# One gate load in another pool with one more bank, and the up part begun seven pairs ahead in a written order

## The chip, the cores and the metric

The kernel runs on one core of one Trainium2 chip. The metric is the device time of one execution in microseconds (us). Engines run side by side: PE multiplies matrices, ACT (ScalarE) and DVE (VectorE) do elementwise work, POOL a little more of it, and SP issues most transfers. Each engine takes its instructions in order, and so does the queue from which SP issues. PE writes into PSUM, which has eight banks here, four under the name "at" and four under "mm"; everything else is in the on-chip memory SBUF or in DRAM.

## The reference

One decoder block in float32 on 1024 tokens (S) of 1024 features (D). What bears on the change:

```python
h = _rmsnorm(x, g_mix_pre)
proj = h @ w_in + b_in                       # u_pool, q, k, v, gates
...
g = sigmoid(gates)                           # 2048 columns
merged = g_pool * (y_pool @ w_branch_pool) + g_attn * (y_attn @ w_branch_attn)
x = x + _rmsnorm(merged @ w_out, g_mix_post)
h2 = _rmsnorm(x, g_mlp_pre)
ff = square(relu(h2 @ w_up)) @ w_down        # 4096 columns between
x = x + _rmsnorm(ff, g_mlp_post)
```

## The kernel before

**Three passes for one product.** A float32 operand is split into a high and a low part (`split`, L99): ACT casts the high part (L101), DVE subtracts it from the source (L104). A product of two operands is then three passes on PE: high by high, high by low, low by high. Wherever a text here says that an operand is made, that is one ACT cast and one DVE subtraction, after the sums that it needs.

**Pairs.** The gates (8 pairs) and the up part of the MLP (16 pairs) work on pairs of 128-column blocks of the weight, an even and an odd one, by a scheme with seven products of half size for eight (`Pairs`, L439). For pair p the products are numbered 1 to 7. `load` (L448) brings one block of weights, by default into a `stage` tile (pool "st", 3 buffers), else into the tile that is given. `operand(p, i)` (L453) makes weight operand i: 1 and 2 from the even block alone, 4 from the odd one, 5, 6, 7 and 3 after sums and differences on DVE (L459, L462, L466, L469). Operands lie in "wh" (6 buffers); 5, 6 and 7 of later pairs in "ga" (gates, 6 buffers) or "x1" (up part, 4 buffers). `mm` (L482) runs one product: 4 column groups by 3 passes, 12 matmuls into one bank. `m1` (L489) runs product 1 and copies the bank out on ACT (L493); `m2` (L495) adds product 2 on the same bank and closes it (a DVE multiplication in the gates, L675; an ACT Relu in the up part, L1071). `rest` (L500) runs 6, 7, 5, 4, 3 and adds on DVE what each gives (L507, L514, L518, L521 or L524, L527). In `rest`, product 4 is added onto the bank of product 7, and then may start only when DVE has read that bank (L514); if a bank `b4` is given, product 4 has that bank to itself and L524 adds it. Product 3 is added onto the bank of product 5 after L518 has read it.

**Order.** Instructions are put in order when the kernel is built: a list scheduler places each one by the order of the program and by when it expects its inputs. Inside a `manual_schedule` block the named engines keep the written order of the block's own instructions; others from outside the block can still be put between them.

**Gates.** Products 1 and 2 of all eight pairs come first, in a block that orders PE, DVE, ACT and SP (L852-L879), while DVE builds the four sums of the activations (T1 to T4) for the column groups kt = 1, 2, 3 (`build_gate`, L702) into "g" tiles (17 buffers). It also loads both blocks of pair 0. The loop at L892 then runs `rest` for p = 0 to 7; it loads the blocks of pair p at its head, the odd block into a "g" tile from p = 3 on and into a stage tile before. `rest(0)` writes into a fresh "y" tile (4 buffers) whose last holder is the result of a pair's products 1 and 2, stored to DRAM at L846.

**Output projection.** `out_mm(n)` (L996) multiplies token block n = 0 to 7 by `w_out`, 48 matmuls into two banks. `out_post(n)` (L1009) is the first norm (ACT squares at L982, then a chain of single-column operations, L1018 and L1019 on DVE) and stores x1; `out_norm(n)` (L1023) is the second, again with L982, and ends with L1027. The result x1 of a block stays in an "x1" tile. At n = 5 `build_first` (L1038) transposes blocks 0 to 3 on PE (L1035, eight groups of four into an "at" bank) and makes operands B11 and B21 from them; an ACT copy (L1045) keeps each group in float32.

**Start of the up part.** From L1157: pairs 0 to 4 are begun ahead (NF0 = 5). `build_second(kt)` (L1048) transposes blocks 4 to 7 for one column group (eight transposes, two banks), and from two banks makes T1 to T4 and B22: one ACT copy (L1056), four DVE operations (L1057-L1060) and five operands. The rest of pair 0 has products 6 and 7 interleaved by column group (`first_kt`), and its result is the tile `f_first`. This part has no written order. After it the loop at L1193 runs pairs 1 to 15: operands, the loads of the next pair, `m1` where it was not run ahead, `flush()` (the stores of the pair before), `rest`. A store (`store`, L1080) is four DVE operations (L1085-L1088) and three transfers to `f_dram`.

**Down part.** From L1322 the squares come back from `f_dram` for the last product. Its gain is `gfin_b` (L1138).

Of the kernel before, what the change touches and what calls it, by code (L numbers as in the profile page):

```python
# [14 lines left out]
P = 128  # L15
# [35 lines left out]
def block_kernel(ctx: ExitStack, tc, xt, x, consts, vecs, sinks, b_qkv, g_post, g_mlp, g_mlp_post,  # L51
# [16 lines left out]
    def nm(s):  # L68
        cnt[0] += 1
        return f"{s}_{cnt[0]}"  # L70
# [618 lines left out]
    def gate_result():  # L689
        return flat(yy.tile([P, 2, 512], F32, tag="y", name=nm("z")))  # L690
# [161 lines left out]
    with tc.manual_schedule(engines={mybir.EngineType.PE, mybir.EngineType.DVE, mybir.EngineType.Activation,  # L852
                                     mybir.EngineType.SP}):
        builds = later_builds()
        gt.load(6)
        gt.load(8)
        load_x(2, lambda: g32([S]))
        first(0)
        first(1)
        for p in range(NG0):  # L860
            if p + 3 < NG0:
                gt.operand(p + 3, 1)
            if p + 2 < NG0:
# [12 lines left out]
            if p + 5 < NG0:  # L876
                gt.load(2 * p + 10)
            elif p < 5:
                gt.load(p - 3)  # L879
    asp = [[None, None], [None, None]]  # L880

    def load_attn():
# [9 lines left out]
    for p in range(8):  # L892
        if NHELD <= p + 1 < 8:
            gt.f0[p + 1] = gate_result()
            nc.sync.dma_start(gt.f0[p + 1], z_dram[2 * p + 2])
        if p:
            gt.load(2 * p)
            gt.load(2 * p + 1, g32([NK, P]) if p > 2 else None)
        for i in (6, 7, 5, 4, 3) if p else (5, 4, 3):
            gt.operand(p, i)  # L900
        tag = "at" if p % 2 == 0 else "mm"
        gt.rest(p, gate_result(), bank(tag), bank(tag), bank(tag), then=load_attn if p == 7 else None)


    def gate_load(m):
# [103 lines left out]
    def out_post(n):  # L1009

        bs = obs.pop(n)
        xs = stage([D])
        nc.sync.dma_start(xs, x[n])
        t = xq.tile([P, D], F32, tag="x1", name=nm("x1"))
        r = mean_sq(bs, halves(t))
        for dj in range(2):
            sl = slice(dj * 512, (dj + 1) * 512)
            dve.scalar_tensor_tensor(t[:, sl], bs[dj], r, gpost_b[:, sl], ALU.mult, ALU.mult)  # L1018
        dve.tensor_tensor(t, t, xs, ALU.add)  # L1019
        nc.sync.dma_start(x1_dram[n], t)  # L1020
        hs[n] = t, xs
# [13 lines left out]
            pe.transpose(b[:, i, :], hs[4 * th + i][:, k * P:(k + 1) * P], ident)  # L1035
        return flat(b)

    def build_first():  # L1038
        for kt in range(4):
            raw[kt] = g32([2, 512])  # L1040
            for h, name in ((0, "B11"), (1, "B21")):
                b = tr_block(0, 4 * h + kt)
                t = gr([2, 512])
                split(t[:, 0, :], t[:, 1, :], b)
                act.copy(raw[kt][:, h, :], b)  # L1045
                X[name][kt] = t

    def build_second(kt):  # L1048
        b12, b22 = tr_block(1, kt), tr_block(1, 4 + kt)
        if kt % 2:  # L1050
            tmp = stage([2, 512])
        else:
            tmp = ga_.tile([P, 2, 512], F32, tag="ga", name=nm("tt"))
        r11, r21 = raw[kt][:, 0, :], raw[kt][:, 1, :]
        t3, t2 = tmp[:, 0, :], tmp[:, 1, :]
        act.copy(t3, b12)  # L1056
# [18 lines left out]
    def up_close0(m, f):  # L1075
# [4 lines left out]
        def store():  # L1080

            g = f_odd.pop(m + 1)
            t = g32([2, 512])
            s4 = bcp.tile([P, 1024], F32, tag="bc", name=nm("s4"))[:, :512]
            dve.tensor_tensor(t[:, 0, :], f[:, 512:], g[:, 512:], ALU.add)  # L1085
            dve.tensor_tensor(t[:, 1, :], t[:, 0, :], f[:, :512], ALU.subtract)
            dve.tensor_tensor(f[:, 512:], f[:, :512], f[:, 512:], ALU.subtract)
# [32 lines left out]
    out_norm(1)  # L1120
    for n in range(2, NT):
        if n == 5:
            out_mm(n, range(0))
            build_first()
            out_mm(n, range(0, NK))
        else:
            out_mm(n, range(NK))
        out_post(n)
        out_norm(n)
        if n == 5:  # L1130
            for p in range(3):
# [22 lines left out]
        h, dj = B_OF[name]  # L1154
        return w_rows[s_, h][:, :, dj * 512:(dj + 1) * 512]

    up.prepare(3)  # L1157
    up.prepare(4)
    up.load(0)
    up.load(1)  # L1160
    for p in range(4):
        up.m1(p, bank("mm"))

    def first_kt(kt):
        up.mm(b6, 0, 6, (kt,))
        up.mm(b7, 0, 7, (kt,))

    build_second(0)
    up.m2(0)
    up.m1(4, bank("mm"))  # L1170
    build_second(1)
    up.operand(0, 6)
    up.m2(1)
    b6, b7 = bank("at"), bank("at")
    build_second(2)
    for i in (7, 5, 4, 3):
        up.operand(0, i)
    up.m2(4)
    up.m2(2)
    first_kt(0)  # L1180
    build_second(3)
    up.m2(3)
    first_kt(1)
    first_kt(2)
    first_kt(3)
    def load_pair(p):
        up.load(2 * p)
        up.load(2 * p + 1, g32([NK, P]))
# [4 lines left out]
    for p in range(1, NP):  # L1193
# [257 lines left out]
```

## Time and profile before

| | |
|---|---|
| runs | 1133.22 us median of 3 (1132.43 to 1134.31) |
| profiled execution | 1132.83 us, its span 1131.0 us |
| mean granted PE clock | 0.998 |
| instructions | 13992 |
| DVE busy | 817.1 us (72%) |
| ACT busy | 523.3 us (46%) |
| DMA | 186.94 MB, mean 165 GB/s |

A row of the timeline has the start from the span's beginning, the time from the first start to the last end, engine, line, operation, tiles (out<-in) and count; in brackets, how long the engine was idle just before, and what released it. A row of windows has, for each engine, its busy time in that stretch and the number of instructions that touch it. "SPq" is a transfer being issued; a count on such a row spreads over its whole time. PE is the matmul, PEld the load of its stationary operand. A matmul's end is modelled, about 0.16 us after the next one may start, so the distance between starts says more than the busy time.

### The profile page before, as it was taken

To read this page: it belongs to the slowest core of one execution; us is meant where nothing else is said; L and a number is where in the kernel's file an instruction comes from. 1 tells how busy PE (TensorE), PEld (TensorE's weight loads), DVE (VectorE), ACT (ScalarE), POOL (GpSimd) and SP (SyncE) were. 2 spreads that over 40 slices of the span, in tenths; PEclk is the share of its full clock that TensorE was granted. 3 is DMA by queue.
4 is the path that set the end of the run, shared out by engine and by line. 5 is a ranking of instruction groups with operands and counts; after the bars stand their busy time and mean duration, and the time that the engine had idled before them with its cause. 6 is when DMAs were issued, how large, how long until landed. Compare 5 with 4: busy or idle time off the path is not lost.

```text
span 1131.0 us, 13992 instructions
## 1 busy us (share of the span) xinstructions
PE 1119.4 (99%) x5213; PEld 925.8 (82%) x5213; DVE 817.1 (72%) x1217; ACT 523.3 (46%) x911; POOL 50.1 (4%) x104
## 2 busy tenths in 40 slices
PE   9999999999999999999999999999999999999997
PEld 8888888878888888888788888888888888888885
DVE  7578897898855785678997666666557955446787
ACT  8265655454432333446555444444444345344342
POOL 0242100000000320000000000000000000000000
PEclk9999999999999999999999999999999999999999
DMA  8102338255664434243365343434597765332652
GB/s 282 50 1 93 113 130 316 100 207 213 224 230 142 162 136 150 97 146 112 141 223 205 138 161 144 157 142 161 214 345 260 244 206 193 100 95 73 223 191 89
DMA packets 72052, 186.94 MB, mean 165 GB/s; under 512 B 6448, under 2 KB 10672, under 8 KB 71984
## 3 DMA queue, kind: packets, MB, share of 16 engines
q1 hardware_dynamic: 66368, 166.38, 42.1%
q10 hardware_dynamic: 5616, 19.66, 4.5%
q8 instruction: 41, 0.67, 0.2%
q14 instruction: 27, 0.22, 0.1%
HBM read 132.54 MB, written 53.48 MB: 164 GB/s over the span
## 4 chain that ended last, share of the span: by engine, by line
PE 92%; DVE 5%; ACT 2%; DMA 1%; issue 1%; DVEq 0%
PE mm L486 22%; PE at L486 15%; PE at L1289 14%; PE mm L1289 12%; PE mm L1006 6%; PE mm L423 5%; PE mm L576 4%; PE mm L183 3%; PE mm L425 3%; PE at L395 2%; PE sc L334 1%; PE at L192 1%; PE sc L183 1%; PE at L1006 1%; PE mm L192 1%; PE at L377 1%
## 5 line engine op out<-in xcount | busy, mean ns | idle before, releaser
L1289 PE MATMUL at<-ar,wh 128*128 128x512 f32 x744 | 169.5, 389 | 0.0
L1289 PEld LDWEIGHTS at<-ar,wh 128*128 128x128 f32 x744 | 139.6, 188 | 29.3 <-DVE ar L104 0.4
L1289 PE MATMUL mm<-ar,wh 128*128 128x512 f32 x576 | 131.0, 389 | 0.0
L104 DVE TENSOR_TENSOR wh<-raw,wh 128x1024 fp32r<-128x1024 f32 x53 | 64.8, 1223 | 86.4 <-ACT wh L101 86.4
L1289 PEld LDWEIGHTS mm<-ar,wh 128*128 128x128 f32 x576 | 108.1, 188 | 22.5
L101 ACT CAST wh<-raw 128x1024 fp32r<-128x1024 f32 x53 | 55.8, 1053 | 135.6 <-PE at L1289 63.3
L101 ACT CAST wh<-st 128x512 fp32r<-128x512 f32 (+1 forms) x105 | 66.2, 642 | 110.4 <-PE at L486 31.0
L104 DVE TENSOR_TENSOR wh<-st,wh 128x512 fp32r<-128x512 f32 (+1 forms) x106 | 79.1, 757 | 21.2 <-ACT wh L101 18.7
L486 PE MATMUL mm<-gr,wh 128*128 128x512 f32 x300 | 72.3, 390 | 0.1
L486 PE MATMUL mm<-T,wx 128*128 128x512 f32 x288 | 67.5, 389 | 0.0
L486 PEld LDWEIGHTS mm<-gr,wh 128*128 128x128 f32 x300 | 56.0, 188 | 11.9 <-ACT g L1071 0.5
L486 PEld LDWEIGHTS mm<-T,wx 128*128 128x128 f32 x288 | 54.1, 188 | 11.2
L486 PE MATMUL at<-T,wx 128*128 128x512 f32 x252 | 59.1, 389 | 0.0
L486 PEld LDWEIGHTS at<-T,wx 128*128 128x128 f32 x252 | 47.3, 188 | 9.8
L486 PE MATMUL mm<-x,wh 128*128 128x512 f32 x240 | 55.2, 389 | 0.0
L486 PEld LDWEIGHTS mm<-x,wh 128*128 128x128 f32 x240 | 45.0, 188 | 9.4
L104 DVE TENSOR_TENSOR ar<-B,ar 128x1024 fp32r<-128x1024 f32 x37 | 45.1, 1219 | 5.6 <-ACT ar L101 5.3
L576 PE MATMUL mm<-x,wh 128*128 128x512 f32 x192 | 47.6, 396 | 0.0
L486 PE MATMUL at<-gr,wh 128*128 128x512 f32 x183 | 44.6, 390 | 0.0
L101 ACT CAST ar<-B 128x1024 fp32r<-128x1024 f32 x37 | 38.9, 1051 | 7.8 <-DMA B<-in_w_dn_dram 4.9
L576 PEld LDWEIGHTS mm<-x,wh 128*128 128x128 f32 x192 | 35.3, 188 | 7.7
L486 PEld LDWEIGHTS at<-gr,wh 128*128 128x128 f32 x183 | 34.3, 188 | 7.7 <-DVE gr L104 0.5
(367 smaller groups left out, 2163.2 us busy)
## 6 DMA issues: line engine op xcount, KB each, us to landing
raw<-f_dram SPq DMA_DIRECT2D x53, 512.0 KB, 3.6
f_dram<-g SPq DMA_DIRECT2D x30, 512.0 KB, 3.3
B<-in_w_dn_dram SPq DMA_DIRECT2D x24, 512.0 KB, 6.3
st<-in_w_up_dram SPq DMA_DIRECT2D x22, 512.0 KB, 3.5
st<-in_w_g_dram SPq DMA_DIRECT2D x19, 512.0 KB, 3.5
f_dram<-g ACTq DMA_DIRECT2D x17, 512.0 KB, 2.6
g<-spill_dram SPq DMA_DIRECT2D x16, 512.0 KB, 4.5
raw<-in_w_dn_dram SPq DMA_DIRECT2D x16, 512.0 KB, 4.5
```

The source lines that it names most:

```text
L101: act.copy(hi, src)
L104: eng.tensor_tensor(lo, src, f32(hi), ALU.subtract)
L183: pe.matmul(bq, xs_[k][n // 4][:, xh, n % 4 * P:(n % 4 + 1) * P], wq[k][:, h, :], start=k == 0 and j == 0, stop=k == NK - 1 and j == 2)
L192: pe.matmul(bkv_of(n), xs_[k][n // 4][:, xh, n % 4 * P:(n % 4 + 1) * P], wkv[k // 2][:, h, k % 2, :], start=k == 0 and j == 0 and not (joi ...
L334: pe.matmul(sb[:, kv, i, :nk], qt[r, qx, m * P:(m + 1) * P], kx[r, k0:k0 + nk], start=j == 0, stop=j == 2)
L395: pe.matmul(yb.rearrange("p m q -> p (m q)"), v[:, vh, kv * HD:kv * HD + P], p[ph][:, 4 * kv:4 * kv + 4].rearrange("p i q -> p (i q)"), st ...
L423: pe.matmul(bs[th], whi[:, k, :], rhs(k, hl, th), start=k == 0 and hl == 0, stop=False)
L425: pe.matmul(bs[th], wlo[:, k, :], rhs(k, 0, th), start=False, stop=k == nk - 1)
L486: pe.matmul(b, w[:, wh, kt, :], xo[kt][:, xh, :], start=not after and kt == 0 and j == 0, stop=kt == 3 and j == 2, skip_group_check=after)
L576: pe.matmul(b, (whi, wlo)[h][:, k, :], xr(k, xh, th), start=j == 0, stop=j == len(mms) - 1)
L1006: pe.matmul(obs[n][dj], l, wos[k][whl][:, dj * 512:(dj + 1) * 512], start=k == 0 and hl == 0 and whl == 0, stop=k == NK - 1 and hl == 1)
L1289: pe.matmul(bs[t], fo[fh][:, k2, t * P:(t + 1) * P], wo_[wh][:, k2, :], start=not after and s2 == 0 and k2 == 0 and j == 0, stop=s2 == NS ...
```

## The change

Gates: both blocks of pair 1 are loaded inside the ordered block at p = 6, the odd one into a "g" tile; the loop no longer loads them. Product 4 of pair 0 has a bank of its own.

Output projection: x1 of block 4 lies in a "g" tile instead of an "x1" tile. At n = 5 the matmuls and the transposes alternate, one eighth of each at a time, in written order on PE. The even block of pair 3 is loaded at n = 6, and the norms of block 7 move into the new block below.

Up part: pairs 0 to 6 are begun ahead (NF0 = 7). Everything from the norms of block 7 to products 6 and 7 of pair 0 is in one block with a written order for PE, DVE and ACT; SP is left to the scheduler. The first results of pairs 4 and 5 lie in "bc" tiles, whose former holder `gfin_b` is loaded after the loop. Transposes and building are two functions, and the building always takes its scratch tile from "ga". In the loop the stores of the pair before come after `rest`; the scratch `s4` of pairs 0 to 6 lies in a "g" tile.

```diff
@@ gates, ordered block
             elif p < 5:
                 gt.load(p - 3)
+            elif p == 6:
+                gt.load(2)
+                gt.load(3, g32([NK, P]))
@@ gates, loop
-        if p:
+        if p > 1:
             gt.load(2 * p)
             gt.load(2 * p + 1, g32([NK, P]) if p > 2 else None)
...
-        gt.rest(p, gate_result(), bank(tag), bank(tag), bank(tag), then=load_attn if p == 7 else None)
+        gt.rest(p, gate_result(), bank(tag), bank(tag), bank(tag), then=load_attn if p == 7 else None,
+                b4=None if p else bank("mm"))
@@ out_post
-        t = xq.tile([P, D], F32, tag="x1", name=nm("x1"))
+        t = g32([D]) if n == 4 else xq.tile([P, D], F32, tag="x1", name=nm("x1"))
@@ build_first: now one group of four transposes, build_first(kt, h)
@@ build_second
-        b12, b22 = tr_block(1, kt), tr_block(1, 4 + kt)
-        if kt % 2:
-            tmp = stage([2, 512])
-        else:
-            tmp = ga_.tile([P, 2, 512], F32, tag="ga", name=nm("tt"))
+    def tr_second(kt):
+        return tr_block(1, kt), tr_block(1, 4 + kt)
+
+    def build_second(kt, b12, b22):
+        tmp = ga_.tile([P, 2, 512], F32, tag="ga", name=nm("tt"))
@@ store
-            s4 = bcp.tile([P, 1024], F32, tag="bc", name=nm("s4"))[:, :512]
+            s4 = (g32([S]) if m < 2 * NF0 else bcp.tile([P, S], F32, tag="bc", name=nm("s4")))[:, :512]
@@ output projection, n == 5 and after
-            out_mm(n, range(0))
-            build_first()
-            out_mm(n, range(0, NK))
+            with tc.manual_schedule(engines={mybir.EngineType.PE}):
+                for k in range(NK):
+                    out_mm(n, (k,))
+                    build_first(k // 2, k % 2)
...
-        out_post(n)
-        out_norm(n)
+        if n < NT - 1:
+            out_post(n)
+            out_norm(n)
...
+        if n == 6:
+            up.load(6)
@@ up part
-    gfin_b = bcast(g_mlp_post, D)
-    NF0 = 5
+    NF0 = 7
-    (pairs 3 and 4 prepared, loads 0 and 1, m1 of 0 to 3, then builds, m2 and m1 of 4 without a written order)
+    def m1_late(p):
+        up.m1(p, bank("mm"), bcp.tile([P, S], F32, tag="bc", name=nm("f0")) if p < 6 else None)
+    with tc.manual_schedule(engines={mybir.EngineType.PE, mybir.EngineType.DVE, mybir.EngineType.Activation}):
+        out_post(NT - 1)
+        up.load(8)
+        up.load(10)
+        up.m1(0, bank("mm"))
+        up.operand(3, 1)
+        up.m1(1, bank("mm"))
+        up.operand(3, 2)
+        out_norm(NT - 1)
+        up.m1(2, bank("mm"))
+        up.operand(4, 1)
+        up.m1(3, bank("mm"))
+        up.operand(4, 2)
+        up.load(0)
+        up.load(1)
+        up.load(12)
+        tr = tr_second(0)
+        build_second(0, *tr)
+        up.m2(0)
+        up.operand(5, 1)
+        tr = tr_second(1)
+        up.m2(1)
+        up.operand(5, 2)
+        build_second(1, *tr)
+        m1_late(4)
+        tr = tr_second(2)
+        up.m2(2)
+        up.operand(0, 6)
+        up.operand(0, 7)
+        m1_late(5)
+        tr3 = tr_second(3)
+        up.m2(3)
+        up.operand(6, 1)
+        up.operand(6, 2)
+        build_second(2, *tr)
+        up.m2(4)
+        m1_late(6)
+        build_second(3, *tr3)
+        up.m2(5)
+        b6, b7 = bank("mm"), bank("mm")
+        first_kt(0)
+        up.m2(6)
+        for i in (5, 4, 3):
+            up.operand(0, i)
+        for kt in range(1, 4):
+            first_kt(kt)
@@ up part, loop over pairs
-        flush()
         up.rest(p, g32([S]), bank(tag), bank(tag), bank(tag))
+        stores.pop(0)()
     flush()
+    gfin_b = bcast(g_mlp_post, D)
```

More of the change, by code (lines that the diff above doesn't have):

```diff
@@ L1036, in tr_block, with build_first @@
         return flat(b)
-    def build_first():
-        for kt in range(4):
+    def build_first(kt, h):
+        if h == 0:
             raw[kt] = g32([2, 512])
[L1041 to L1048, printed above, removed]
-        b12, b22 = tr_block(1, kt), tr_block(1, 4 + kt)
-        if kt % 2:
-            tmp = stage([2, 512])
-        else:
-            tmp = ga_.tile([P, 2, 512], F32, tag="ga", name=nm("tt"))
+        b = tr_block(0, 4 * h + kt)
+        t = gr([2, 512])
+        split(t[:, 0, :], t[:, 1, :], b)
+        act.copy(raw[kt][:, h, :], b)
+        X["B21" if h else "B11"][kt] = t
+    def tr_second(kt):
+        return tr_block(1, kt), tr_block(1, 4 + kt)
+    def build_second(kt, b12, b22):
+        tmp = ga_.tile([P, 2, 512], F32, tag="ga", name=nm("tt"))
         r11, r21 = raw[kt][:, 0, :], raw[kt][:, 1, :]
@@ L1155, in w_block @@
         return w_rows[s_, h][:, :, dj * 512:(dj + 1) * 512]
[L1157 to L1162, printed above, removed]
+    def m1_late(p):
+        up.m1(p, bank("mm"), bcp.tile([P, S], F32, tag="bc", name=nm("f0")) if p < 6 else None)
     def first_kt(kt):
```

18 lines of the change are left out of this document (removed).

## The prediction

> **What bounds the kernel now.** First the page, then the chain in order of time, then windows around the places where the chain leaves PE.
>
> ```profile
> span 1131.0 us, 13992 instructions
> PE 1119.4 (99%) x5213; PEld 925.8 (82%) x5213; DVE 817.1 (72%) x1217; ACT 523.3 (46%) x911; POOL 50.1 (4%) x104
> st<-in_w_up_dram SPq DMA_DIRECT2D x22, 512.0 KB, 3.5
> 568.48 13.60 PE at L486 x60
> 218.35:234.68 16.33, 15.24 (x64) 11.36 (x62) 13.73 (x23) 7.25 (x13) 0.00 (x0) 1.00 0.40 144
> 471.12:485.86 14.74, 14.55 (x80) 11.72 (x79) 10.58 (x21) 12.33 (x26) 0.00 (x0) 1.00 0.21 72
> 508.06:518.95 10.89, 10.89 (x50) 8.96 (x49) 7.66 (x19) 6.26 (x16) 0.00 (x0) 1.00 0.51 169
> 518.95:554.72 35.77, 34.43 (x165) 27.86 (x164) 34.21 (x56) 22.63 (x42) 0.00 (x0) 1.00 0.23 82
> 556.00:818.00 262.00, 262.00 (x1158) 216.89 (x1157) 187.04 (x289) 122.53 (x181) 0.00 (x0) 1.00 0.47 176
> 818.00:1112.00 294.00, 294.00 (x1298) 243.15 (x1297) 192.69 (x194) 127.12 (x152) 0.00 (x0) 1.00 0.56 187
> ```
>
> PE is the bound, and the number of matmuls does not change. Sixty matmuls in 13.60 us give 0.2267 us each. So the change can win only the time in which PE waits. From 556 to 1112 there is none (busy equals the stretch), and three stretches remain: the start of the gates' `rest` (218.35 to 234.68), block 5 with its transposes (471 to 486), and the start of the up part (518.95 to 554.72). In the last, DVE is busy 34.21 of 35.77 us: PE and DVE limit it together.
>
> **Gates.**
>
> ```profile
> 210.20 0.42 SPq L450 DMA_DIRECT2D g<-in_w_g_dram  x1
> 220.32 2.49 DVE L104 TENSOR_TENSOR gr<-xr,gr 128x512 fp32r<-128x512 f32 x4
> 222.73 1.28 DVE L675 TENSOR_TENSOR z<-mm,rb_all 128x512 f32<-128x512 f32 x2
> 225.00 2.23 PE L486 MATMUL at<-gr,wh 128*128 128x512 f32 x9
> 225.24 21.62 SPq L450 DMA_DIRECT2D st<-in_w_g_dram  x6
> 226.94 0.69 DVE L514 TENSOR_TENSOR z<-z,at 128x512 f32<-128x512 f32 x1 [0.52 <-DMA spill_dram<-z]
> 227.73 0.69 DVE L518 TENSOR_TENSOR z<-z,at 128x512 f32<-128x512 f32 x1
> 227.78 0.93 PE L486 MATMUL at<-T,wh 128*128 128x512 f32 x3 [0.55 <-DVE z L514]
> 229.68 0.69 DVE L459 TENSOR_TENSOR ws<-st 128x512 f32<-128x512 f32 x1 [1.26 <-DMA st<-in_w_g_dram]
> 233.34 0.84 PE L486 MATMUL mm<-T,ar 128*128 128x512 f32 x3
> 234.68 0.50 PE L486 MATMUL mm<-T,ar 128*128 128x512 f32 x1 [0.50 <-DVE ar L104]
> 235.02 2.22 PE L486 MATMUL mm<-gr,ar 128*128 128x512 f32 x9
> ```
>
> 63 matmuls start here and take 14.28 us; the stretch lasts 16.33, so 2.05 are lost. Product 4 of pair 0: nine matmuls from 225.00 end at 227.04, the next starts at 227.78 after L514, which itself waited for the store of the old "y" tile: 0.74, and 0.08 to refill. A bank of its own takes this wait away; the late L514 then delays only L518, which ends at 228.4, and product 3, whose bank L518 reads, is due a product (2.72) after 226.84 or so, at 229.56: covered. L524 replaces L521, no DVE work is added, and its bank is one of the four "mm" banks, whose last readers are the two L675 that end at 224.0.
>
> Pair 1: three matmuls from 233.34 end at 234.02, the next starts at 234.68: 0.66 and 0.11 to refill. Behind it is the odd block of pair 1, whose stage tile came free at 225.24; it landed 4.4 us later, when L459 starts. In a "g" tile it can go at about 210.2, where the row shows another odd block (pair 3's) take the free one; what is late next is pair 3's: it gets the tile that pair 1 gives back before its product 4 (three products after 232.5, 240.7), lands 4.4 later and is wanted at 232.5 + 2 x 13.6 = 259.7. From L459 to the operand are three DVE steps and a cast, some 2.7 us; begun after L518 at 228.4, with one other step between, they end by 231.8, and PE now asks at 232.5. The two loads are the last that the ordered block puts on SP, so nothing of it waits behind them. So I take 1.59 - 0.09 = **1.5 us** gained. The other 0.46 (the last build, 220.32) stays.
>
> **Block 5.**
>
> ```profile
> 471.12 1.91 PE L1035 MATMUL at<-cst,x 128*128 128x128 f32 x16
> 472.78 0.71 PE L1006 MATMUL mm<-wohi,gr 128*128 128x512 f32 x2
> 476.88 0.66 PE L1035 MATMUL at<-cst,x 128*128 128x128 f32 x4 [0.18 <-ACT g L1045]
> 479.32 0.60 ACT L982 ACTIVATE x<-mm 128x512 f32<-128x512 f32 x1
> ```
>
> Sixteen transposes in 1.66 us are 0.104 each; 32 take 3.32, 48 matmuls 10.88, together 14.20 of 14.74: 0.54 lost, where PE asks for a bank that L1045 has not yet copied. After, a group comes every 1.36 + 0.42 us and has four banks, 7 us, for cast, subtraction and copy (three steps of 0.6 to 0.7). L982 of block 4, which now waits until the transposes free its "x1" tile (479.32), moves some 8 us earlier into this stretch; ACT is busy 12.33 of 14.74 with it counted, so the banks cover it. Eight re-entries for five cost about 0.09. Gain **0.45 us**.
>
> **Start of the up part.**
>
> ```profile
> 513.68 0.63 ACT L982 ACTIVATE st<-x 128x512 f32<-128x512 f32 x1 [1.59 <-DVE x L1019]
> 517.00 1.28 DVE L1027 SCALAR_TENSOR_TENSOR x<-x,rr,bc 128x1024 f32<-128x1024 f32 x1
> 518.95 1.03 PE L1035 MATMUL at<-cst,x 128*128 128x128 f32 x8
> 519.74 2.98 PE L486 MATMUL mm<-gr,wh 128*128 128x512 f32 x12
> 523.35 6.08 PE L486 MATMUL mm<-gr,wh 128*128 128x512 f32 x24
> 524.85 0.60 ACT L1071 ACTIVATE g<-mm 128x512 f32<-128x512 f32 x1
> 525.50 3.50 PEld L486 LDWEIGHTS mm<-gr,wh 128*128 128x128 f32 x16 [0.50 <-ACT g L1071]
> 526.38 0.68 DVE L1057 TENSOR_TENSOR g<-at,g 128x512 f32<-128x512 f32 x1
> 529.27 1.03 PE L1035 MATMUL at<-cst,x 128*128 128x128 f32 x8
> 531.50 0.68 DVE L104 TENSOR_TENSOR T<-g,T 128x512 fp32r<-128x512 f32 x1
> 539.00 1.52 PE L486 MATMUL at<-T,wh 128*128 128x512 f32 x6
> 540.70 0.73 PE L486 MATMUL at<-T,wh 128*128 128x512 f32 x2 [0.18 <-ACT wh L101]
> 548.77 1.97 PE L486 MATMUL mm<-T,wh 128*128 128x512 f32 x8
> 551.83 3.06 PE L486 MATMUL at<-ar,wh 128*128 128x512 f32 x12 [1.08 <-DVE f_first L518]
> ```
>
> Three waits: 24 matmuls from 523.35 end at 528.79, the next row is at 529.27 (0.48, behind L1071); six from 539.00 end at 540.36, next 540.70 (0.34); eight from 548.77 end at 550.58, next 551.83 (1.25). With 0.11 of refill for the last two, 2.29.
>
> The written order puts 48 more matmuls (products 1 and 2 of pairs 5 and 6, 10.9 us) before 554.72, and on DVE only four more subtractions of 0.60 spacing. I walked the written order with these rows: a product 2.72, eight transposes 0.79, a cast 0.62, a DVE step 0.60, a build 5.8 on DVE (526.38 to 532.18).
>
> *PE*: `m1` of pairs 0 to 3 as now, 508.06 to 518.95; `m2(0)` 519.8, `m2(1)` 523.4, `m1(4)` 526.1, `m2(2)` 529.7, `m1(5)` 532.4, `m2(3)` 536.0, `m2(4)` 538.7, `m1(6)` 541.4, `m2(5)` 544.1, column group 0 of products 6 and 7 546.8, `m2(6)` 548.2, groups 1 to 3 from 550.9, product 5 at 555.0, with the four groups of transposes at 518.95, 522.5, 528.8 and 535.1.
>
> *The norm of block 7*: ACT must first copy `m1(1)` (ends 508.06 + 24 x 0.2267 = 513.50) and make a cast, so L982 starts at 514.7 to 514.9, not 513.68. L1027 starts 3.32 and ends 4.60 after it, at 519.3 to 519.5; the first transpose of block 7, fourth in its group, is asked for at 518.95 + 3 x 0.104 = 519.3. The cover is used up; 0 to 0.2 us.
>
> *DVE*: build 0 ends at 526.4 as now. Operand (5,1) to 527.0. (5,2) has its cast behind the Relu of `m2(1)`, which needs PE's 526.1, so it ends at 528.0; build 1 to 533.8. Operand (0,6): two sums, a cast, a subtraction, to 536.4; (0,7) one sum, a cast, a subtraction, to 538.3. The casts of (6,1) and (6,2) stand behind the Relu of `m2(3)`, PE's 538.7: 538.9 + 0.6 + 0.6 + 0.7 = 540.8 for (6,1), 541.3 for (6,2). Build 2 to 547.1 and build 3 to 552.9, operand (0,5) to 553.5.
>
> *What PE asks and when it is there*: (6,1) at 541.4, there at 540.8. The bank of b7 at 547.5; ACT frees it with the Relu of `m2(4)`, behind the casts of build 2, at 546.0. T2 and T3 of group 3 at 553.6, there 1.2 us before build 3 ends, 551.7. (0,5) at 555.0, there 553.5. The transposes' banks come free with the builds, 2 us and more before they are asked for. *Loads*: pair 6's goes when (5,2) gives its stage tile back, 528.0, lands 3.5 later and is wanted by ACT at 539.5; if it were late, every cast and Relu behind it on ACT would be too.
>
> So the walk shows no wait but the 0 to 0.2: gain **2.29 us**. `first_kt`'s product 5 then comes long after L514, where 1.25 were lost.
>
> The trace of before has no such hand-offs, so the three tight ones ((6,1) with 0.6 us, block 7 with none, b7 with 1.5) are bounded by nothing and by three waits like the worst here, 3 x 1.36 = 4.1 us. They can't gain more than the waits already counted. I take 0.4, near the low end, since the walk has two of them on time.
>
> At nothing: stores after `rest` (DVE is free 75 of 262 us after 556; uncovered, 4 x 0.6 per pair), seven pairs at 13.6 us instead of five (18 DVE steps of 0.6, 10.8 us; the row from 556 on holds four such pairs without a wait), `s4` in "g", and `gfin_b` later (not read before the third product).
>
> **Sum**: -1.5 - 0.45 - 2.29 + 0.4 = -3.84 on 1132.83 (span 1131.0 and 1.83 around it) is 1129.0. The median lies 0.39 above this execution: **1129.4**.
>
> **Rivals.**
>
> *The order on ACT works against PE* (slower). ACT must do the Relus and copies that wait for PE between the casts that PE waits for. It already happens: `m2(0)` ended at 519.74 + 2.72 = 522.46, its Relu came only at 524.85, while ACT worked on build 0, and PE waited for it at 525.50. From the Relu of `m2(3)` on, five hand-offs follow in a row. If ACT is late there by over 0.6 us, operand (6,1), build 2, `m1(6)`, build 3 and operand 5 each wait; at 1.36 each 6.8 us, less 4.2 gained: +2.6, 1135.8. Against it: ACT is busy only 22.63 of 35.77. The Trainium skill, "PSUM — Partial Sum Buffer", section "Engine vs sequencer instructions", states that ScalarE and VectorE queues are strict FIFO, which speaks against a written order that is wrong in one place; the late Relu at 524.85 agrees.
>
> *The earlier load feeds DVE at the wrong time.* L459 and L462 of pair 1 could be put ahead of the last build (220.32), for which PE already waits: 2 x 0.69 = 1.4 lost again, 1132.83 - 2.44 + 0.39 = 1130.8. DVE is busy 13.73 of 16.33 there, which speaks for it.
>
> *The up part doesn't get shorter*, because builds on DVE set its end and pairs 5 and 6 only fill PE elsewhere: without 2.29, 1131.7. Against: DVE's 34 us and 2.4 more now lie beside 45 us of PE.
>
> **How the numbers follow.** Forecast 0.61 (own range 1128.2 to 1130.7), DVE in the gates 0.13, no gain in the up part 0.11, ACT's order 0.15. Low end: all 4.9 us of waits gone, less 0.8 of spread between runs, 1127.8; high end: gains lost to the bound of 4.1, and some spread, 1133.4. About 0.2% (2.3 us, below 1130.9 or above 1135.5) can be told from no change; a part of each middle rival is faster, and of the last not slower: faster 0.70, same 0.18, slower 0.12.
>
> **What would show it.** Right: the product after 226.8 starts unbroken, L459 of pair 1 waits for no DMA; no PE idle behind L1045; `first_kt` and product 5 unbroken, and pair 1 of the up part starting 10.9 less 4.2 us later than 554.72. Wrong: PE idle behind ACT L1071 or DVE L104 of "wh" between 519 and 556, at block 7's transposes, or anywhere after 563, where I expect none.

## The result, and the profile after

| | median | lowest to highest | profiled execution |
|---|---|---|---|
| before | 1133.22 us (5 runs) | 1132.43 to 1134.31 | 1132.83 |
| after | 1128.44 us (5 runs) | 1127.89 to 1129.03 | 1128.25 |

The ratio of the times is 0.9956, with a 95% interval of 0.9942 to 0.9969: 4.8 us faster. The forecast was 1129.4 us, between 1127.8 and 1133.4. In the kernel after the squares of the norms are L986, the last step of a norm L1031, the transposes L1039, the operations of a build L1058 to L1062, the Relu L1073, the stores' operations L1087 to L1090.

The page of the kernel after, its first rows:

```profile
span 1126.4 us, 13987 instructions
PE 1117.5 (99%) x5213; PEld 926.7 (82%) x5213; DVE 814.5 (72%) x1217; ACT 524.5 (47%) x911; POOL 50.1 (4%) x104
```

The same windows as before, moved to where these stretches now lie (columns as before: stretch, its length, then busy time and instructions of PE, PEld, DVE, ACT, POOL, the granted clock, DMA share, GB/s):

```profile
218.39:233.09 14.70, 14.65 (x65) 11.72 (x64) 13.81 (x23) 8.31 (x14) 0.00 (x0) 1.00 0.41 144
469.44:483.64 14.20, 14.20 (x78) 11.74 (x77) 12.19 (x28) 11.22 (x27) 0.00 (x0) 1.00 0.45 149
506.00:560.00 54.00, 54.00 (x256) 45.02 (x255) 45.81 (x81) 33.69 (x68) 0.00 (x0) 1.00 0.29 98
560.00:814.00 254.00, 254.00 (x1122) 210.41 (x1121) 181.86 (x285) 120.39 (x172) 0.00 (x0) 1.00 0.50 180
```

All three stretches are full now: PE's busy time equals their length, but for 0.05 us in the gates (a matmul that starts a little late still counts as busy). The number of matmuls is the same, 5213, and the granted clock is 1.00 in all these windows. So the starts of the same matmul in the two traces, counted from 0, say where the time went:

| from matmul to matmul | what lies there | before | after | difference |
|---|---|---|---|---|
| 1209 to 1400 | start of the gates' `rest` | 45.47 | 43.68 | -1.79 |
| 1400 to 2300 | up to block 5 | 204.34 | 204.37 | 0.03 |
| 2300 to 2400 | block 5 and transposes | 19.72 | 19.17 | -0.55 |
| 2500 to 2800 | start of the up part | 66.61 | 64.35 | -2.25 |
| 2800 to 5212 | all the rest | 546.98 | 547.01 | 0.03 |

Three places, and what they gave still stands at the end (last matmul 1123.23 before, 1118.76 after). The timeline of the gates, after:

```profile
210.24 0.42 SPq L450 DMA_DIRECT2D g<-in_w_g_dram  x1
226.37 0.68 DVE L459 TENSOR_TENSOR ws<-g 128x512 f32<-128x512 f32 x1
227.62 2.20 PE L486 MATMUL mm<-gr,wh 128*128 128x512 f32 x9
229.66 2.88 PE L486 MATMUL at<-x,wh 128*128 128x512 f32 x12
232.38 0.84 PE L486 MATMUL mm<-T,ar 128*128 128x512 f32 x3
```

Product 4 goes into an "mm" bank. L459 of pair 1 has no bracket (it waits for no DMA) and its operand `ar` is there when PE asks. PE in the up part, after:

```profile
505.81 11.05 PE L486 MATMUL mm<-gr,wh 128*128 128x512 f32 x48
533.80 11.14 PE L486 MATMUL mm<-gr,wh 128*128 128x512 f32 x48
548.85 4.24 PE L486 MATMUL mm<-T,wh 128*128 128x512 f32 x18
552.93 2.88 PE L486 MATMUL at<-T,wh 128*128 128x512 f32 x12
561.09 4.24 PE L486 MATMUL mm<-T,wx 128*128 128x512 f32 x18
```

No row has a bracket, so PE waits nowhere in them. Pair 1 of the up part starts at 561.09, where 554.72 + 10.9 - 4.2 = 561.4 was expected.

### The profile page after: what moved, and what is told of

Same layout as the page of the kernel before. It is cut to its first block, busy times and chain, and to the rows that moved or that the text cites. A ratio compares the mean times of both kernels' runs of the same rounds, so it can differ in the third digit from the quotient of the medians.

```text
span 1126.4 us, 13987 instructions
## 1 busy us (share of the span) xinstructions
PE 1117.5 (99%) x5213; PEld 926.7 (82%) x5213; DVE 814.5 (72%) x1217; ACT 524.5 (47%) x911; POOL 50.1 (4%) x104
## 4 chain that ended last, share of the span: by engine, by line
PE 97%; DVE 2%; ACT 1%; issue 0%; DVEq 0%
PE mm L486 24%; PE at L486 15%; PE at L1323 14%; PE mm L1323 12%; PE mm L1010 7%; PE mm L423 5%; PE mm L576 4%; PE mm L183 3%; PE mm L425 3%; PE at L395 2%; PE sc L334 1%; PE at L192 1%; PE sc L183 1%; PE at L1010 1%; PE mm L192 1%; PE at L1039 1%
## 5 line engine op out<-in xcount | busy, mean ns | idle before, releaser
L104 DVE TENSOR_TENSOR wh<-raw,wh 128x1024 fp32r<-128x1024 f32 x53 | 64.8, 1223 | 88.2 <-ACT wh L101 88.0
L104 DVE TENSOR_TENSOR wh<-st,wh 128x512 fp32r<-128x512 f32 (+1 forms) x105 | 78.3, 756 | 35.6 <-ACT wh L101 32.9
L486 PE MATMUL mm<-gr,wh 128*128 128x512 f32 x333 | 79.3, 390 | 0.0
L486 PEld LDWEIGHTS mm<-gr,wh 128*128 128x128 f32 x333 | 62.2, 188 | 12.7
L104 DVE TENSOR_TENSOR ar<-B,ar 128x1024 fp32r<-128x1024 f32 x37 | 45.1, 1219 | 3.7 <-ACT ar L101 3.3
L486 PE MATMUL at<-gr,wh 128*128 128x512 f32 x150 | 36.6, 390 | 0.0
L486 PE MATMUL mm<-T,wh 128*128 128x512 f32 x147 | 36.1, 389 | 0.0
```

The source lines that it names most:

```text
L104: eng.tensor_tensor(lo, src, f32(hi), ALU.subtract)
L486: pe.matmul(b, w[:, wh, kt, :], xo[kt][:, xh, :], start=not after and kt == 0 and j == 0, stop=kt == 3 and j == 2, skip_group_check=after)
```

## The experiments

Each kernel ran on one chip with runs of the kernel before beside it; the chip is not the same for all. All times in us:

| run | median | kernel before, beside it | ratio, 95% interval |
|---|---|---|---|
| gates_bank | 1135.91 | 1133.69 | 1.0019, 1.0010 to 1.0028 |
| gates_load | 1132.96 | 1133.69 | 0.9995, 0.9986 to 1.0003 |
| gates_only | 1131.03 | 1133.69 | 0.9976, 0.9966 to 0.9986 |
| block5_only | 1132.89 | 1133.69 | 0.9992, 0.9983 to 1.0001 |
| block5_nog | 1138.41 | 1133.37 | 1.0049, 1.0034 to 1.0064 |
| up_only | 1131.49 | 1133.37 | 0.9989, 0.9980 to 0.9999 |
| no_order | 1128.84 | 1133.37 | 0.9962, 0.9949 to 0.9975 |
| five_ordered | 1134.04 | 1133.37 | 1.0005, 0.9996 to 1.0015 |
| six_ordered | 1129.51 | 1134.05 | 0.9961, 0.9946 to 0.9976 |
| dup4 | 1130.13 | 1134.05 | 0.9967, 0.9954 to 0.9980 |
| flush_first | 1131.52 | 1134.05 | 0.9981, 0.9971 to 0.9991 |
| early_build | 1131.42 | 1134.05 | 0.9977, 0.9968 to 0.9987 |

The first two parts below, and up_only, put one part of the change into the kernel before. The others take something out of the kernel after, or put something in, and are read against its 1128.44. The kernel after did not run beside them, and the median of the kernel before moved from 1133.22 (beside the kernel after) to 1133.37 and 1134.05, so differences of medians below about 1 us say little here. The traces are firmer. From matmul 1200 to the last one, the kernel after and no_order, whose matmuls come in the same order, agree to 0.01 us; over the kernel after, the traces of dup4, six_ordered, flush_first, early_build and five_ordered take 1.98, 1.55, 3.00, 4.57 and 5.88 us more.

### Gates: the bank alone, the load alone, both

gates_bank, on the kernel before:

```diff
-        gt.rest(p, gate_result(), bank(tag), bank(tag), bank(tag), then=load_attn if p == 7 else None)
+        gt.rest(p, gate_result(), bank(tag), bank(tag), bank(tag), then=load_attn if p == 7 else None,
+                b4=None if p else bank("mm"))
```

> The kernel before with only a bank of its own for product 4 of pair 0 in the gates. Theory (waits follow each other on PE, and the later one swallows what the earlier one gives): PE reaches pair 1 some 0.8 us earlier, but the operand of pair 1 still waits for its odd block, which lands 4.4 us after the stage tile comes free at 225.24, so product 6 of pair 1 stands at 234.7 as before and the total changes by 0 to -0.2 us. Rival (the waits add up one by one, as the prediction's sum priced them): -0.82 us by itself, about 1132.4.

gates_load, on the kernel before:

```diff
+            elif p == 6:
+                gt.load(2)
+                gt.load(3, g32([NK, P]))
...
-        if p:
+        if p > 1:
             gt.load(2 * p)
```

> The kernel before with only the early load of pair 1's blocks in the gates (the odd one into a g tile). Theory: the wait for the odd block (0.66 and 0.11 to refill) goes and the wait of product 4 behind L514 stays: -0.77 us, about 1132.4, and L459 of pair 1 waits for no DMA. Rival (L459 and L462 of pair 1 are put ahead of the last build): +0.6, as 1.4 us of DVE work comes in front of the gr operands at 220.3.

gates_only has both diffs.

> The kernel before with both parts of the gates and nothing else. Theory: both waits go, and the sum of the two parts is more than what each gives alone: -1.6 to -1.8 us, about 1131.5, and the 1400th matmul of the trace starts 1.7 us earlier. Rival: the two parts add up (the same -1.6), which can be told only by the two runs of one part. A second rival, that the gain is taken back by a later wait: 0.

Both together won 2.7 us by the medians, more than the 1.6 to 1.8 expected. The bank alone lost 2.2, which neither theory had, and the load alone won 0.7 or nothing. (The profiled execution of gates_bank is the shortest of its eleven, 1134.38; the seven longest are those with a mean granted clock of 0.996 or 0.997, so a part of the 2.2 may be the clock.) Two rows each of DVE and PE of gates_bank:

```profile
234.33 0.68 DVE L469 TENSOR_TENSOR st<-st,st 128x512 f32<-128x512 f32 x1
239.69 0.69 DVE L459 TENSOR_TENSOR ws<-st 128x512 f32<-128x512 f32 x1 [1.94 <-DMA st<-in_w_g_dram]
```

```profile
232.78 0.73 PE L486 MATMUL mm<-T,ar 128*128 128x512 f32 x2 [0.67 <-ACT ar L101]
237.81 0.50 PE L486 MATMUL mm<-T,ar 128*128 128x512 f32 x1 [0.93 <-DVE ar L104]
```

PE is earlier by the bank and then waits for pair 1's operand all the same, as the theory had it. What it had not: DVE's order changed with the edit. L469, which gives pair 1's odd stage tile back, now comes at 234.33, behind three operations (L686, L104 and L527) that it preceded in the kernel before, where it ran at 232.21. The load of the next pair goes out that much later, L459 of pair 2 waits 1.94 us for it, and PE waits again at 237.81. In gates_load DVE's order changed as well, one pair later:

```profile
256.47 0.69 DVE L459 TENSOR_TENSOR ws<-g 128x512 f32<-128x512 f32 x1 [3.74 <-DMA g<-in_w_g_dram]
258.28 0.68 DVE L518 TENSOR_TENSOR z<-z,at 128x512 f32<-128x512 f32 x1
```

```profile
227.24 0.93 PE L486 MATMUL at<-T,wh 128*128 128x512 f32 x3 [0.73 <-DVE z L514]
259.11 3.00 PE L486 MATMUL at<-x,wh 128*128 128x512 f32 x12 [1.66 <-DVE z L518]
```

The wait behind L514 is still there, as expected. But L459 of a later pair, which nobody needs yet, stands on DVE ahead of L518 of pair 2 and waits 3.74 us for its block; product 3 needs L518, and PE loses 1.66. With both edits the scheduler put L459 behind L518. So the gains of the two parts alone don't add up to what they give together.

Why did both together give 2.7, and the traces of before and after only 1.79? The runs block5_only, up_only and block5_nog, described below, have the gates of the kernel before unchanged. The timeline of pair 1's odd block, its issue and L459, in block5_only and then in up_only:

```profile
225.23 1.22 SPq L450 DMA_DIRECT2D st<-in_w_g_dram  x2
230.43 0.69 DVE L459 TENSOR_TENSOR ws<-st 128x512 f32<-128x512 f32 x1 [2.45 <-DMA st<-in_w_g_dram]
```

```profile
224.91 0.93 SPq L450 DMA_DIRECT2D st<-in_w_g_dram  x2
230.34 0.69 DVE L459 TENSOR_TENSOR ws<-st 128x512 f32<-128x512 f32 x1 [2.05 <-DMA st<-in_w_g_dram]
```

| trace | issue to L459 | wait at product 4 | matmul 1209 to 1400 | less issue to L459 |
|---|---|---|---|---|
| before | 229.68 - 225.24 = 4.44 | 0.71 | 45.47 | 41.03 |
| block5_only | 5.20 | 0.28 | 46.22 | 41.02 |
| up_only | 5.43 | 0.92 | 46.45 | 41.02 |
| block5_nog | 5.43 | 0.86 | 46.45 | 41.02 |

(The wait is the distance of the two starts less 0.23.) The stretch is the landing time of one transfer plus a constant, to 0.02 us, whatever PE lost at product 4. So in the kernel before one wait set the gates, not two: the one at product 4 was swallowed by the next. It comes up once the load is early: in gates_load PE still loses 0.89 there. The profiled execution of before happened to have the quickest of the four landings. With the change the landing is off the path, and the stretch is 43.68, and 43.67 in gates_only: 1.79 to 2.77 less, 2.5 on average over the four. The spread of the times was small too, 1130.39 to 1131.36 for gates_only; but no_order, which has the same gates, went from 1127.98 to 1129.98, so the landing is not shown to be all of the spread.

### Block 5: with and without the tile for block 4

block5_only has the diff's hunk for n == 5, the split `build_first(kt, h)`, and:

```diff
-        t = xq.tile([P, D], F32, tag="x1", name=nm("x1"))
+        t = g32([D]) if n == 4 else xq.tile([P, D], F32, tag="x1", name=nm("x1"))
```

> The kernel before with only block 5 and its transposes interleaved in written order and the x1 of block 4 in a g tile. Theory: the 0.54 us in which PE asked for a bank that L1045 had not yet copied go, -0.45 to -0.55 us, about 1132.7, and all of it still stands at the last matmul. Rival (the start of the up part is set by DVE, so that an earlier PE waits there instead): 0 at the end, with 0.5 more of waits between 519 and 555.

Matmul 2300 to 2400 took 19.17 us, 0.55 less than before and just what the whole change takes; matmul 2500 to 2800 took 66.63 (before 66.61), so the up part took nothing of it back. block5_nog has the rest of that and leaves this line as it was before:

```diff
-        t = g32([D]) if n == 4 else xq.tile([P, D], F32, tag="x1", name=nm("x1"))
+        t = xq.tile([P, D], F32, tag="x1", name=nm("x1"))
```

> The kernel before with block 5 and its transposes interleaved in written order, but x1 of block 4 left in an x1 tile. Theory (that tile comes free only after the last transpose, some 13 us later than where it was, so L982 of block 4 and the two banks that it empties are late, and block 6 finds no bank): PE waits 3 to 4.5 us before block 6, total 2.5 to 4 over the kernel before. Rival (the g tile is not needed, the banks are covered either way): 0.5 less than before, as with it.

It lost 5.0 us. The operations of the norm of block 4, and PE:

```profile
486.00 0.60 ACT L982 ACTIVATE x<-mm 128x512 f32<-128x512 f32 x1 [0.19 <-PE at L1035]
```

```profile
490.09 1.45 PE L1006 MATMUL mm<-wohi,gr 128*128 128x512 f32 x2 [3.79 <-DVE x L1018]
491.33 1.05 PE L1006 MATMUL mm<-wolo,gr 128*128 128x512 f32 x2
492.19 1.05 PE L1006 MATMUL mm<-wohi,gr 128*128 128x512 f32 x2
493.04 0.70 PE L1006 MATMUL mm<-wohi,ar 128*128 128x512 f32 x2
```

L982 waits for the last transpose, and block 6 for the bank: 3.79, as expected. The rest of the 5 us was not expected: after the wait two matmuls take 0.86 us instead of 0.45 (491.33 to 492.19 to 493.04), because the granted clock has fallen; that is told below. The tile for block 4 is thus no detail: the interleaving needs it.

### The up part alone, its order, its number of pairs

up_only, on the kernel before, is the change without the hunks of the gates, of block 5 and of `out_post`; its core:

```diff
-    NF0 = 5
+    NF0 = 7
...
+    with tc.manual_schedule(engines={mybir.EngineType.PE, mybir.EngineType.DVE, mybir.EngineType.Activation}):
+        out_post(NT - 1)
...
-        flush()
         up.rest(p, g32([S]), bank(tag), bank(tag), bank(tag))
+        stores.pop(0)()
```

> The kernel before with only the up part of the change (block 7's norms and seven pairs in one written order, the stores after rest, s4 and gfin_b moved), gates and block 5 as before. Theory (the three waits of 2.29 us go, nothing new comes): 2.0 to 2.3 us less than the kernel before, and in the trace the 2500th to the 2800th matmul take 64.4 us instead of 66.6. Rival (DVE's builds set the end of this stretch): 0 to -0.5, with PE waiting before the first products 6 and 7.

Matmul 2500 to 2800 took 64.35 us, 2.25 less than before, as expected, and the median is 1.9 less. Later, at 615, PE loses 0.30 in this trace, which the kernel after does not; the cause is told under flush_first.

no_order, on the kernel after:

```diff
-    with tc.manual_schedule(engines={mybir.EngineType.PE, mybir.EngineType.DVE, mybir.EngineType.Activation}):
+    if True:
         out_post(NT - 1)
```

> The changed kernel with the written order of the up part given up: the same instructions, loads, tiles and seven pairs, but PE, DVE and ACT placed by the scheduler. Theory A (the order takes the waits away, the seven pairs alone don't, since the Relus and casts can again fall behind the builds on ACT and DVE): at least 1 us over the changed kernel, 1129.4 or more, with PE waits behind ACT or DVE between 505 and 562. Theory B (two more pairs ahead are cover enough in any order): within 0.4 of the changed kernel, 1128.0 to 1128.9.

Theory B, by the trace. PE's order is the same without being forced; DVE's and ACT's are not (the operations of build 2 are mixed in among the operands of pairs 0 and 6, all of which come before it in the written order), and PE still waits nowhere:

```profile
506.00:560.00 54.00, 54.00 (x256) 45.04 (x255) 46.30 (x82) 32.94 (x67) 0.00 (x0) 1.00 0.29 98
```

The last matmul starts at 1118.75, 0.01 from the kernel after. The median is 0.4 higher, and two of the five runs took 1130.0, over the highest of the kernel after (1129.03); the trace is of one of the others, 1128.24. In it, binding DVE and ACT to the written order gives nothing by itself; the scheduler keeps near the order of the program, and that is the new one either way.

five_ordered, on the kernel after (all loads, operands and products of pairs 5 and 6 go out of the block):

```diff
-    NF0 = 7
+    NF0 = 5
...
-        up.load(10)
...
-        up.operand(5, 1)
...
-        m1_late(5)
...
-        up.m2(5)
```

> The changed kernel with the written order kept but with five pairs ahead instead of seven: no loads, operands and products 1 and 2 of pairs 5 and 6 ahead. They are then made in the loop as for the later pairs. Theory (DVE needs its 34 us for the builds, and PE has 10.9 us less to do beside them): PE comes to the column groups 2 and 3 of products 6 and 7 before build 3 is done (about 545), waits 3 to 5 us there, and the total is 3 to 5 over the changed kernel, 1131.5 to 1133.5. Rival (the order alone was the gain): within 0.5 of the changed kernel.

It lost 5.6 us, more than expected. PE:

```profile
542.99 0.49 PE L486 MATMUL mm<-T,wh 128*128 128x512 f32 x1 [2.51 <-ACT T L101]
544.13 0.98 PE L486 MATMUL mm<-T,wh 128*128 128x512 f32 x3 [0.65 <-DVE T L104]
545.34 1.22 PE L486 MATMUL mm<-T,wh 128*128 128x512 f32 x2 [0.23 <-DVE T L104]
546.35 1.05 PE L486 MATMUL at<-T,wh 128*128 128x512 f32 x2
547.21 1.05 PE L486 MATMUL mm<-T,wh 128*128 128x512 f32 x2
548.06 2.19 PE L486 MATMUL at<-T,wh 128*128 128x512 f32 x8
```

The waits come to 2.51 + 0.65 + 0.23 = 3.4, where they were expected, behind the casts and subtractions of builds 2 and 3; what is over is again matmuls at 0.43 instead of 0.23 (546.35 to 548.06: four in 1.71). The written order alone is thus no gain: with five pairs ahead, matmul 2500 to 2800 takes 70.37 us in it, and 66.61 in the kernel before, which the scheduler ordered.

six_ordered, on the kernel after, in the same way:

```diff
-    NF0 = 7
+    NF0 = 6
...
-        up.load(12)
...
-        up.operand(6, 1)
-        up.operand(6, 2)
...
-        m1_late(6)
...
-        up.m2(6)
```

> The changed kernel with six pairs ahead instead of seven (NF0 = 6), all else in the written order. Theory (five were short by 4.0 us of waits, a sixth pair puts 5.4 us on PE and only 1.2 on DVE): no wait over 0.5 us, and within 0.5 of the changed kernel, 1128.0 to 1128.9; the seventh pair is then a reserve, not a gain. Rival (the builds end too late for six as well): a PE wait of 1.5 to 2.5 us before column group 3, 1130 or more.

```profile
546.68 0.96 PE L486 MATMUL mm<-T,wh 128*128 128x512 f32 x3 [0.27 <-DVE T L104]
547.88 0.73 PE L486 MATMUL mm<-T,wh 128*128 128x512 f32 x2 [0.24 <-DVE T L104]
```

1.1 us over the kernel after by the medians, between the theory and its rival: two waits at build 3's operands, 0.51 us of idle time together. With the matmuls behind them, which also start late by up to 0.13 each, matmul 2600 to 2700 takes 1.5 us more than in the kernel after. So the pairs ahead are the lever: 1134.04, 1129.51, 1128.44 with five, six and seven. That the seventh counts rests on the trace, since beside their runs of the kernel before six and seven differ little (ratios 0.9961 and 0.9956).

dup4, on the kernel after, in `operand`:

```diff
             split(t[:, 0], t[:, 1], src)
+            if self.src is w_up and (p, i) == (6, 1):
+                for _ in range(4):
+                    dve.tensor_tensor(t[:, 1], src, t[:, 0], ALU.subtract)
```

> The changed kernel with the low part of operand (6,1) subtracted four more times, so that (6,1) and all DVE work behind it come 4 x 0.60 = 2.4 us later. Theory (PE is the bound and the walk's cover of 0.6 is real; the later hand-offs shift with PE, so the delay is paid once): product 1 of pair 6, asked for at 539.24, starts 1.8 later, no second wait follows, and the total is 1.8 to 2.1 over the changed kernel, about 1130.3. Rival (ACT's order works against PE, each of the hand-offs behind it waits by itself): several PE waits between 539 and 556, 4 us or more. Second rival (the cover is much larger than the walk said): under 0.5.

```profile
532.96 6.15 PE L489 MATMUL mm<-gr,wh 128*128 128x512 f32 x26
540.76 5.32 PE L489 MATMUL mm<-gr,wh 128*128 128x512 f32 x22 [1.65 <-DVE wh L476]
```

```profile
537.11 0.69 DVE L104 TENSOR_TENSOR wh<-st,wh 128x512 fp32r<-128x512 f32 x1 [1.70 <-ACT wh L101]
537.84 2.87 DVE L476 TENSOR_TENSOR wh<-st,wh 128x512 fp32r<-128x512 f32 x4
```

The median is 1.7 over that of the kernel after, the trace 1.98, and there is one wait, no second one: the delay is paid once, since every later hand-off moves with PE. The rows also give the cover more exactly. The low part ends at 540.71 instead of 537.80, 2.91 later, and PE loses 1.81 (its starts lie 2.04 apart there instead of 0.23); so the cover was 1.1 us, not 0.6. The first row shows why: 26 matmuls come before the wait, 24 of product 2 of pairs 3 and 4 and two of product 1 of pair 6. The low part of the weight is wanted by the third pass only, 2 x 0.227 later than the walk had it.

flush_first, on the kernel after:

```diff
+        flush()
         up.rest(p, g32([S]), bank(tag), bank(tag), bank(tag))
-        stores.pop(0)()
```

> The changed kernel with the stores of the pair before put ahead of rest again, as in the kernel before. Theory (DVE has the room from 556 on, the move was costed at nothing): within 0.3 of the changed kernel. Rival (the four DVE operations of each store stand ahead of sums that free a bank, and the move was needed): at least 0.6 us more for one pair, 1129.0 or more, with PE waits behind DVE after 563.

The rival: 3.1 us over the kernel after, 3.00 in the trace.

```profile
590.23 0.69 DVE L459 TENSOR_TENSOR ws<-g 128x512 f32<-128x512 f32 x1 [2.54 <-DMA g<-in_w_up_dram]
597.45 0.69 DVE L1090 TENSOR_TENSOR g<-g,g 128x512 f32<-128x512 f32 x1
598.05 0.69 DVE L514 TENSOR_TENSOR g<-g,mm 128x512 f32<-128x512 f32 x1
```

```profile
598.79 3.04 PE L486 MATMUL mm<-T,wh 128*128 128x512 f32 x12 [0.50 <-DVE g L514]
```

All four operations of the store stand ahead of L514, which frees the bank for product 4; PE waits there in four pairs in a row (583, 598, 613 and 628), 0.2 to 0.7 us each and 2.0 together. In the kernel after, L514 of that pair runs at 594.83, ahead of the first of them. The order is not the whole cause. In the kernel before all four also stand ahead of L514 in two pairs (L514 at 588.46 and 603.26), and PE does not wait: there L459, the first sum of the next pair, began 2.8 and 0.8 us before PE began the pair. Here it waits for its load and begins 1.2 to 2.3 us after that (590.23, the pair at 588.38). In the kernel after it begins 2.0 to 2.8 us after, and the stores behind L514 leave room for it.

This room is small, and up_only and early_build, which have the same up part, ran out of it in one pair (the fourth of the loop). In the kernel after L459 begins 2.0 us after PE began that pair, and PE loses nothing; in up_only 3.5 us, after 2.62 of waiting for the load, and PE loses 0.30; in early_build 4.3 us, after 3.42 of waiting, and PE loses 1.10.

### The wait that is left in the gates

early_build, on the kernel after, makes the four splits of the last build one pair sooner:

```diff
-            if 1 <= p <= 6:
+            if 1 <= p <= 5:
                 next(builds)
...
             if p == 5:
+                next(builds)
                 gt.operand(0, 6)
```

> The changed kernel with the four splits of the last gate build made one pair earlier (after product 2 of pair 4, not of pair 5). Theory (the last wait of the gates, 0.2 to 0.3 us at 220.7 behind the gr operands of that build, goes and nothing else is late): 0.2 to 0.3 less than the changed kernel, 1128.1. Rival (the earlier splits stand ahead of the sums and of operands 6 and 7 on ACT and DVE, or wait for g tiles, and PE waits in the last pairs of products 1 and 2 instead): 0.5 or more over it.

The rival: 3.0 over the kernel after.

```profile
219.45 0.73 PE L486 MATMUL at<-T,wh 128*128 128x512 f32 x2 [1.04 <-ACT wh L101]
220.73 0.50 PE L486 MATMUL at<-T,wh 128*128 128x512 f32 x1 [0.55 <-DVE wh L104]
```

The splits now stand ahead of operand 6 of pair 0, and PE waits for that one instead, twice. In this trace, the longest of the ten runs (1132.65), matmul 1209 to 1400 takes 47.11 us, 3.43 more than in the kernel after. The 1.10 at 614 told above are in the same trace; whether the edit made that load late is not shown. No kernel here is faster than the kernel after.

## Why the prediction was right

**The bound** was right: PE is busy 99%, and the gain is the idle time that went, at the three places named and nowhere else. What was forecast to be nothing (the rest of the trace) is 0.03 us.

**Gates: 1.5 predicted, 1.79 in the traces, about 2.5 over several executions.** The two waits were priced by the time PE stood idle, 0.82 + 0.77. With both edits that idle time goes, so the sum holds for the trace it was read from; as the price of each edit it does not. In the kernel before the stretch follows the landing of pair 1's odd block alone, so the bank gives nothing until the load is early. The 1.5 became 1.79 in the traces because 0.09 had been taken off without a stated reason, 0.12 was lost just outside the stretch that was summed, and the 0.46 that were to stay are 0.38 (43.68 less 191 x 0.2267). It became 2.5 since one execution was taken for the kernel, the one with the quickest landing: that the forecast lay so near is in part luck.

**Block 5: 0.45 predicted, 0.55 measured.** The step was right, with the banks as the cause and the tile for block 4 as what makes it possible. The 0.09 for more changes between matmuls and transposes did not show: 0.54 were lost before, and 0.55 came back.

**Up part: 2.29 predicted, 2.25 measured.** The walk held. Its tight places had more cover than it gave them. Operand (6,1) had 1.1. The norm of block 7 ends 3.83 after its first square, not 4.60, since less came between its steps:

```profile
512.45 0.64 ACT L986 ACTIVATE st<-x 128x512 f32<-128x512 f32 x1
```

```profile
514.99 1.29 DVE L1031 SCALAR_TENSOR_TENSOR x<-x,rr,bc 128x1024 f32<-128x1024 f32 x1
```

It is there at 516.28; the fourth transpose, which needs it, starts at 517.02. So the allowance of 0.4 for hand-offs was a term too much: the kernel after has no such wait. It is the largest part of the 1.0 us between forecast and median: 0.4 there, 0.3 in the gates, 0.1 in block 5, and 0.2 because the median lies 0.19 over the profiled execution, not 0.39. The low end of the range does not add up by its own terms: 1133.22 less 4.9 and 0.8 is 1127.5, not 1127.8; the shortest run, 1127.89, lies inside either.

**At nothing**: true of the change as it stands, but not for the reason given. That DVE is free 75 of 262 us says nothing of the place where it is needed. The stores' new place was costed as free, and is; flush_first shows that their old place would have taken 3.0 of the gain back. The pair loop did go on unbroken after 563 in the trace of the kernel after, but not in those of up_only (0.30 lost) and early_build (1.10), where a load came later, so the seven pairs at 13.6 us are not free in every execution.

**The rivals.** ACT's order against PE: dup4 shows that a delay there is paid once (PE's start comes 1.81 late, 1.98 with the late start of the next matmuls), not at each of five hand-offs, and the trace of no_order that another order on ACT and DVE costs nothing. DVE taking L459 ahead of the last build: gates_only has the full gain, so not with both edits; with the load alone L459 of a later pair did get ahead of L518 and cost 1.66. The up part not getting shorter: it did, alone and with the rest.

## What to carry to other kernels

Where waits follow each other on the bound engine, taking one away may give nothing: ask of each whether the next one hangs on a transfer or on another engine's time, and if so price them together, and from several traces, for a landing differs from run to run. Where a stretch is limited by two engines at once, work of the bound engine that needs nothing of the other can be brought forward into it; count it pair by pair until the other's time is covered. And a part of an edit that looks like a detail (a tile, the place of a store) may be what the rest stands on: undo it alone before it is called free.

## What the hardware showed besides

After a wait of PE the granted clock falls to half for some microseconds, and not after long waits alone. Windows of block5_nog (one wait of 3.79 us) and of early_build (two of 1.04 and 0.55):

```profile
488.00:490.00 2.00, 0.00 (x0) 0.00 (x0) 1.90 (x7) 1.00 (x2) 0.00 (x0) 0.94 0.00 0
490.00:492.00 2.00, 1.91 (x4) 1.35 (x5) 1.91 (x3) 0.02 (x1) 0.00 (x0) 0.50 0.00 0
492.00:494.00 2.00, 2.00 (x7) 1.58 (x7) 0.31 (x2) 2.00 (x8) 0.00 (x0) 0.70 0.63 250
```

```profile
220.00:222.00 2.00, 1.45 (x6) 1.03 (x6) 2.00 (x5) 0.09 (x1) 0.00 (x0) 0.90 0.00 0
222.00:224.00 2.00, 2.00 (x6) 1.55 (x5) 1.97 (x4) 2.00 (x5) 0.00 (x0) 0.50 0.00 0
224.00:226.00 2.00, 2.00 (x8) 1.59 (x7) 2.00 (x4) 0.61 (x2) 0.00 (x0) 0.74 0.40 154
```

In early_build nine matmuls then take 3.39 us instead of 2.04, so 1.35 of its loss is the clock. A single wait of 1.65 (dup4) or 1.66 us (gates_load) left the clock at 1.00. The Trainium skill, "TensorE: Matmul & The Clock Gate", section "HAM oscillation — how this bites in real kernels", gives as its rule that there be no idle gap of PE over about 3.4 us. The wait of 3.79 agrees with it; the two short waits, 1.6 us of idle within 2.4 us, do not, nor does five_ordered, where waits of 2.51 and 0.65 were enough (clock 0.50 from 546 to 548); the measurement decides. What exactly trips the clock was not settled.

The transfer of one and the same block (pair 1's odd one) took from 4.44 to 5.43 us from issue to use in four traces with the same code around it, and the stretch moved with it to 0.02 us. The chip alone does not explain it: gates_bank and block5_only, on one chip, had 4.63 and 5.20.
